# Expert blocks of 56 slots, convolutions that read PSUM, and a reordered VectorE queue in a two-block transformer kernel

## Chip, cores and metric

The kernel runs on one core of one Trainium2 chip. The metric is device time in microseconds (us) of one execution. TensorE is called PE, VectorE DVE, ScalarE ACT, GpSimd POOL and SyncE, which issues the DMAs, SP, as in the profile.

## What is computed

One sequence of 512 tokens with 1024 features passes two blocks, all in fp32. The first block (gated attention, then retention, each with attention to a memory) is not touched. The second block is a mixer and a mixture of experts:

```python
# mixer: three of the projections feed a short convolution, four a gated delta rule with 4 heads of 128
def causal_dwconv(x, w):                 # depthwise over the 512 tokens, K taps
    xp = jnp.pad(x, ((0, 0), (K - 1, 0), (0, 0)))
    y = xp[:, 0:S] * w[0]
    for j in range(1, K):
        y = y + xp[:, j:j + S] * w[j]
...
y = b * causal_dwconv(c * hx, conv_w)                                  # K = 3
qkv = jax.nn.silu(causal_dwconv(concatenate([q, k, v]), conv_w))       # K = 4
q = q * lax.rsqrt(jnp.sum(q * q, axis=-1) + EPS) * (DN_HEAD_DIM ** -0.5)   # k likewise, no factor
...
# experts: 4 groups of 8, each token goes to 2 experts of its best group
yb = (jax.nn.silu(xblk @ w_gate[e]) * (xblk @ w_up[e])) @ w_down[e]    # 1024 -> 512 -> 1024
out = zeros((N, D)).at[slot_tok].add(yb * slot_gate[:, None])
```

There are 32 experts, so 1024 assignments of tokens. All expert weights (32 times three matrices of 2 MB) are read from HBM once.

## The kernel before, in words

**Delta-rule layer (938 to 1245 us).** `dn` (line 1065 on) works head by head. `dn_head` (L1229) makes one 128x512 projection at a time for k, q and v into one of four PSUM banks (pool `pacc`, L444), each a product in three fp32r parts (hH/hL by wh/wl). `conv` (L1186) first has ACT copy the bank into a padded SBUF tile `cpad` (L1259), which frees the bank; DVE then scales (L1195) and adds three shifted taps (L1197) in `cy`. After the SiLU and a transpose, ACT squares the head (L1271) and DVE sums the squares by token (L1272). `short_conv` (L1200) uses the same `conv` with 3 taps, its input made by a DVE product. In this layer the order on each engine comes from the framework's scheduler.

**Experts (1258 us to the end).** `moe` (L1415) cuts the slots of all experts into 16 pairs; an expert has CAP = 64 slots, so a pair is 128 rows.

- `route` (L1500) computes, for each token, its two slot numbers `dest`.
- `build_S` (L1638) makes one-hot matrices from `dest` on DVE, 128 tokens by 128 slots at a time: a comparison with an iota (L1656) and a second one added (L1657). A "quad" is four experts (256 slots).
- `gather_T` (L1660) multiplies tokens by one-hots: 8 feature blocks, 4 token tiles, high and low part, 64 matmuls of 256 columns, into `mhT`. It runs in every second pair; the first stands before pair 0.
- `slot_rows` (L1699) spreads `dest` over the partitions with 16 matmuls, kept as 16-bit `rows`. `slots` (L1709) makes from them the transposed one-hots `ST` of a pair, two comparisons and two comparisons with addition (L1715, L1716).
- `gates` (L1735) gets the gate weight of each slot: four matmuls of 8 columns against the one-hots and some ten tiny DVE operations.
- `gate_up` (L1758) multiplies one expert's 64 rows with its gate and up weights (32 matmuls of 512 columns in two halves), `act_T` (L1793) transposes and forms h (L1802, L1803), `down` (L1806) multiplies by the down weights in two halves of the pair, `y_out` splits the result, and `combine` adds it to the tokens: 16 matmuls of 512 columns and 8 DVE additions (L1852).
- Weights come in tiles of 1 MB through 18 buffers: NWA = 12 and NWB = 6. SP issues a load when a buffer is free (L1767, L1812).
- `spill` (L1597) makes a table of experts with more than CAP tokens, for `overflow` (L1858), a loop at the end that runs once for each block of the table.

In this stage PE's order is written out (`self.pe = self.ordered(nc.tensor)`). For a pair p it is: gate and up of expert 0; down half 1 of pair p-1; the transposes; first half of gate and up of expert 1; combine of p-1; second half; the gather, if there is one; the gate products of p+1; down half 0; transposes of expert 1. DVE and ACT follow the scheduler, which starts work as early as its operands allow, unless `after(a, b)` (L216) sets a behind b on their engine. `sums` shows what DVE is given at the combine:

```python
def sums():
    if p:
        self.combine(blks[p - 1], [(t, n) for n in range(2) for t in range(NT)])
    self.slots(blks[p])
    if more and p % 2:
        self.build_S(quads[p // 2 + 1])
    if not p:
        ov.extend(self.spill(mc))
```

Of the kernel before, what the change touches and what calls it, by code (L numbers as in the profile page):

```python
# [22 lines left out]
P = 128  # L23
# [12 lines left out]
CAP = 64  # L36
NPAIR = NE // 2
SLOTS = NE * CAP
MAXOV = 16
# [3 lines left out]
NWB = 6  # L43
# [11 lines left out]
CM = ["ones", "iota", "ustrict", "eend", "pcol"]  # L55
# [8 lines left out]
def constants():  # L64
# [4 lines left out]
    c["ones"] = np.ones((P, P))  # L69
# [23 lines left out]
    c["pcol"] = np.stack([i, (i + CAP) % P], 1) - P  # L93
# [30 lines left out]
class Model:  # L124
# [689 lines left out]
    def out_router(self, W, heads):  # L814
# [13 lines left out]
        cm = self.rtp.tile([P, sum(self.off[k][1] for k in CM)], F32, tag="cm", name="cm")  # L828
        nc.sync.dma_start(cm, A["cm"])
        iota = self.const(cm, "iota")  # L830
        self.io3 = rp.tile([P, 2, CAP], F32, tag="io3", name="io3")
        V.tensor_copy(self.io3.rearrange("p a n -> p (a n)"), iota)
# [4 lines left out]
        V.tensor_copy(self.onesb, self.const(cm, "ones"))  # L837
        V.tensor_copy(self.ustb, self.const(cm, "ustrict"))
        V.tensor_copy(self.eend, self.const(cm, "eend"))
        V.tensor_scalar(out=self.e64b, in0=self.eend[0:1, :], scalar1=float(-CAP), scalar2=None, op0=ALU.add)  # L840
        self.pcol = rp.tile([P, 2, NPAIR], F32, tag="pcol", name="pcol")
        ends = self.eend.rearrange("p (n e) -> p n e", e=2)[:, None, :NPAIR, 1]
        nc.gpsimd.tensor_tensor(self.pcol, ends.to_broadcast([P, 2, NPAIR]),
                                self.const(cm, "pcol")[:, :, None].to_broadcast([P, 2, NPAIR]), op=ALU.add)
# [341 lines left out]
    def conv(self, wk, src, width, wv):  # L1186

        nc = self.nc
        V = nc.vector
        pad = width - 1  # L1190
        cp = wk.tile([P, S + 3], F32, tag="cpad", bufs=1, name="cpad")
        V.memset(cp[:, :pad], 0.0)
        src(cp[:, pad:pad + S])
        y = wk.tile([P, S], F32, tag="cy", name="cy")
        V.tensor_scalar(out=y, in0=cp[:, 0:S], scalar1=wv(0), scalar2=None, op0=ALU.mult)  # L1195
        for j in range(1, width):
            V.scalar_tensor_tensor(out=y, in0=cp[:, j:j + S], scalar=wv(j), in1=y, op0=ALU.mult, op1=ALU.add)  # L1197
        return y

    def short_conv(self, wk, ct, Wr, C):  # L1200
# [3 lines left out]
        for i in (2, 0, 1):  # L1204
# [4 lines left out]
        y = self.conv(wk, lambda d: V.tensor_tensor(d, pss[1], c, op=ALU.mult), 3,  # L1209
                      lambda j: aw[:, j * 4 + ct:j * 4 + ct + 1])  # L1210
# [18 lines left out]
    def dn_head(self, wk, h, Wr, C, sc, pre):  # L1229
# [23 lines left out]
        for n, (nm, c0) in enumerate(DNC):  # L1253
# [5 lines left out]
            y = self.conv(wk, lambda d: SC.activation(d, ps, AF.Copy), 4, lambda j: cw[:, j * 12 + ci:j * 12 + ci + 1])  # L1259
# [11 lines left out]
            SC.activation(sq, v4(pt), AF.Square)  # L1271
            V.tensor_reduce(ss[:, n * NT:(n + 1) * NT], sq, axis=AX.X, op=ALU.add)  # L1272
# [142 lines left out]
    def moe(self, psd):  # L1415
# [9 lines left out]
        io3 = self.io3  # L1425
        et = mc.tile([P, NPAIR, 1], F32, tag="et", name="et")
        blks = []
        quads = [dict(base=float(q * 2 * P), io=io3, n=2 * P) for q in range(NPAIR // 2)]
        for p in range(NPAIR):
            w = {}  # L1430
            for j in range(2):
                for n, src in (("g", "w_gate_2"), ("u", "w_up_2"), ("d", "w_down_2")):
                    w[n, j] = A[src][0, 2 * p + j]
            nc.gpsimd.tensor_scalar(out=et[:, p, :], in0=self.hm64[:, 1:2], scalar1=float(2 * p), scalar2=None, op0=ALU.add)
            blks.append(dict(pair=p, quad=quads[p // 2], cols=slice(p % 2 * P, (p % 2 + 1) * P), w=w, n=2,
                             e=et[:, p, :], cut=p == NPAIR - 1))
        nb = NPAIR
        self.quad0 = quads[0]
        self.route(mc)
        for q in quads:  # L1440
            q["dest"] = self.dest
# [5 lines left out]
        self.gather_T(quads[0], True)  # L1447
        self.slot_rows()
        blks[0]["first"] = True
        ov = []  # L1450
        for p in range(nb):
            more = p + 1 < nb

            def sums():
                if p:
                    self.combine(blks[p - 1], [(t, n) for n in range(2) for t in range(NT)])
                self.slots(blks[p])
                if more and p % 2:
# [12 lines left out]
            self.gate_up(blks[p], 1, half=sums if more else lambda: self.act_T(blks[p], 0))  # L1471
            if more:
                if not p:
                    self.act_T(blks[0], 0)
# [20 lines left out]
        self.overflow(mc, wk, io3, gb, ot, *ov)  # L1495

    def route(self, mc):
# [30 lines left out]
        iota = self.io3[:, 0, :]  # L1528
# [32 lines left out]
        self.quad0["dest"] = self.dest = dest  # L1561
        self.rt = (oh, ohf, sl, ge, q, sc[3], onesb)

        self.build_S(self.quad0)
# [30 lines left out]
        G.tensor_tensor(self.gxs[:, :, 4:8], gx, self.gxs[:, :, 0:4].bitcast(F32), op=ALU.subtract)  # L1595

    def spill(self, mc):  # L1597
# [11 lines left out]
        for m in range(2, 8):  # L1609
# [3 lines left out]
        V.memset(ones, 1.0)  # L1613
# [4 lines left out]
        for i in range(MAXOV):  # L1618
            cmp = sc[:, (8 + i % 2) * NE:(9 + i % 2) * NE]
# [18 lines left out]
    def build_S(self, blk):  # L1638
# [3 lines left out]
        S3 = wk.tile([P, NT, 2 * P], F32R, tag="S3", name="S3")  # L1642
        iof = blk["io"].rearrange("p a n -> p (a n)")
        ds = []
        for n in range(blk["n"] // P):
            dest = blk["dest"]
            if n or not isinstance(blk["base"], float) or blk["base"]:
                db = wk.tile([P, 2 * NT], F32, tag=f"db{n}", name="db")
                V.tensor_scalar(out=db, in0=dest, scalar1=blk["base"] + n * P if n else blk["base"], scalar2=None,
                                op0=ALU.subtract)  # L1650
                dest = db
            ds.append(dest)
        for t in range(NT):
            for n, dest in enumerate(ds):
                o = S3[:, t, n * P:(n + 1) * P]
                V.tensor_scalar(out=o, in0=iof, scalar1=dest[:, t:t + 1], scalar2=None, op0=ALU.is_equal)  # L1656
                self.last = V.scalar_tensor_tensor(out=o, in0=iof, scalar=dest[:, NT + t:NT + t + 1],  # L1657
# [3 lines left out]
    def gather_T(self, blk, first=False):  # L1661
# [4 lines left out]
        hT = blk["hT"] = wk.tile([P, KD, 2 * P], F32, tag="mhT", name="mhT")  # L1666
        pss = {}

        def mms(k, t, start):
            if k // 2 not in pss:  # L1670
                pss[k // 2] = self.att()
            o = pss[k // 2][:, k % 2 * 2 * P:k % 2 * 2 * P + n]
            for c, part in enumerate(self.xs):
                self.mm(o, part[:, t, k, :], S3[:, t, :n], start and c == 0,
                        t == NT - 1 and c == 1 and (not first or k % 2 == 1))

        def put(b):
            pv = pss[b].rearrange("p (k n) -> p k n", k=2)[:, :, :n]
            o = hT[:, 2 * b:2 * b + 2, :n]
            if b % 2:  # L1680
                nc.vector.tensor_tensor(o, pv, self.gv[:, 2 * b:2 * b + 2, None].to_broadcast([P, 2, n]), op=ALU.mult)
            else:
                for k in range(2):
                    nc.scalar.activation(o[:, k, :], pv[:, k, :], AF.Copy, scale=self.gv[:, 2 * b + k:2 * b + k + 1])

        if first:
            for t in range(NT):
                for k in range(KD):
                    mms(k, t, t == 0 and k % 2 == 0)
                    if t == NT - 1 and k % 2:  # L1690
                        put(k // 2)
        else:
            for k in range(KD):
                for t in range(NT):
                    mms(k, t, t == 0)
                if k % 2:
                    put(k // 2)

    def slot_rows(self):  # L1699

        self.rows = self.wk.tile([P, 2, S], U16, tag="rows", name="rows")
        for i in range(2):
# [4 lines left out]
            self.nc.vector.tensor_scalar(out=self.rows[:, i, :], in0=ps, scalar1=60000.0, scalar2=None, op0=ALU.min)  # L1707

    def slots(self, blk):  # L1709
# [3 lines left out]
        for s, o in enumerate(blk["ST"]):  # L1713
            c = self.pcol[:, s, blk["pair"]:blk["pair"] + 1]
            V.tensor_scalar(out=o, in0=self.rows[:, 0, :], scalar1=c, scalar2=None, op0=ALU.is_equal)  # L1715
            V.scalar_tensor_tensor(out=o, in0=self.rows[:, 1, :], scalar=c, in1=o.bitcast(F32), op0=ALU.is_equal,  # L1716
                                   op1=ALU.add)

    def slot_T(self, blk):
# [3 lines left out]
        for t in range(NT):  # L1723
            self.tr(ps[:, t * P:(t + 1) * P], self.of(blk, "S3")[:, t, :].bitcast(F32))
        blk["ST"] = [wk.tile([P, S], F32R, tag=f"ST{s}", name=f"ST{s}") for s in range(2)]
        SC.activation(blk["ST"][0], ps, AF.Copy)
        for i in range(2):
            SC.activation(blk["ST"][1][(1 - i) * CAP:(2 - i) * CAP, :], ps[i * CAP:(i + 1) * CAP, :], AF.Copy)

    @staticmethod  # L1730
    def of(blk, name):

        return blk["quad"][name][:, :, blk["cols"]]

    def gates(self, blk):  # L1735
# [4 lines left out]
        S3 = self.of(blk, "S3")  # L1740
        for t in range(NT):
            self.mm(ps[:, :8], S3[:, t, :], self.gxs[:, t, :], t == 0, t == NT - 1)
        a = wk.tile([P, 8], F32, tag="ga", bufs=2, name="ga")
# [4 lines left out]
        gt = wk.tile([P, 4], F32, tag="gt", bufs=2, name="gt")  # L1748
# [235 lines left out]
```

## Time and profile before

| | |
|---|---|
| median of 3 runs | 1773.61 us (1772.92 to 1774.19) |
| profiled execution | 1773.5 us |
| its span | 1771.7 us |
| busy: PE, DVE, ACT, POOL | 1724.4, 1007.2, 590.6, 96.6 us |
| chain that ended last | PE 89%, DVE 6%, ACT 2%, DMA 2% |

The span goes from the first to the last instruction. An engine that is idle costs something only where the chain passes through it. The two stages touched by the change have different limits, so their windows are to be read apart.

### The profile page before, as it was taken

Reading aid. Unit: us, or ns where it says so; the run is one execution under the profiler, and the core shown is the slowest. Engines: PE = TensorE matmul, PEld = TensorE weight load, DVE = VectorE, ACT = ScalarE, POOL = GpSimd, SP = SyncE. Lnnn points to the kernel's source line nnn. Section 1 sums busy time; section 2 is a strip of 40 time slices with the busy share of each in tenths; the row PEclk is TensorE's granted clock in tenths of the full one; section 3 lists DMA queues with packets and bytes.
Section 4 is the critical chain, followed back from the end, with each engine's and each line's share of the span. In section 5 each row is a group of like instructions: output and inputs, shape, how many; then the busy total and the mean of one; then the engine's idle time right before and its main releaser. Section 6 shows DMA issues by size and latency. Waiting matters only on the chain.

```text
span 1771.7 us, 24714 instructions
## 1 busy us (share of the span) xinstructions
PE 1724.4 (97%) x9410; PEld 1255.9 (71%) x9410; DVE 1007.2 (57%) x2660; ACT 590.6 (33%) x1173; POOL 96.6 (5%) x143
## 2 busy tenths in 40 slices
PE   8999999999999999999999999999999999999996
PEld 7888888878888888888888777778644445354443
DVE  7655564563757555454657978875545435453534
ACT  7643333433536232222446433334211111111112
POOL 0000000000000110111011000010200000000001
PEclk9999999999999999999999999999999999999998
DMA  8633233233223322223213342326799999999981
GB/s 260 175 96 90 81 93 95 73 86 96 69 92 99 92 85 82 84 75 103 76 48 81 91 111 62 85 69 265 301 418 418 410 409 420 407 407 407 420 321 49
DMA packets 199276, 318.82 MB, mean 180 GB/s; under 512 B 18789, under 2 KB 159590, under 8 KB 174450
## 3 DMA queue, kind: packets, MB, share of 16 engines
q1 hardware_dynamic: 199154, 317.21, 50.6%
q8 instruction: 75, 1.23, 0.3%
q14 instruction: 47, 0.39, 0.1%
HBM read 312.16 MB, written 5.01 MB: 179 GB/s over the span
## 4 chain that ended last, share of the span: by engine, by line
PE 89%; DVE 6%; ACT 2%; DMA 2%; issue 1%; SPq 0%; POOL 0%; POOLq 0%; ACTq 0%; DVEq 0%
PE acc L143 50%; PE pg L230 13%; PE att L143 8%; PE att L230 7%; PE pd L230 6%; PE trp L148 3%; PE trp L230 1%; PE trp L143 1%; DVE wl L205 1%; ACT wh L204 1%; DMA raw<-in_w_mem_kv_dram 1%; DVE cy L1197 1%; PE att L148 0%; ACT hH L243 0%; DMA kvf<-kvd 0%
## 5 line engine op out<-in xcount | busy, mean ns | idle before, releaser
L205 DVE TENSOR_TENSOR wl<-raw,wh 128x1024 fp32r<-128x1024 f32 x184 | 225.8, 1227 | 189.8 <-ACT wh L204 179.8
L143 PE MATMUL acc<-hH,wh 128*128 128x512 f32 (+1 forms) x760 | 297.3, 392 | 5.4 <-DVE sz L578 3.1
L143 PE MATMUL acc<-hL,wh 128*128 128x512 f32 (+1 forms) x760 | 299.1, 394 | 0.0
L143 PE MATMUL acc<-hH,wl 128*128 128x512 f32 (+1 forms) x760 | 298.0, 392 | 0.0
L204 ACT ACTIVATE wh<-raw 128x1024 fp32r<-128x1024 f32 x184 | 194.6, 1059 | 276.8 <-PE acc L143 262.2
L230 PE MATMUL pg<-mw,mhT 128*64 128x512 f32 x1024 | 230.3, 597 | 0.0
L143 PEld LDWEIGHTS acc<-hH,wh 128*128 128x128 f32 x760 | 143.7, 190 | 31.4 <-DVE sz L578 3.3
L143 PEld LDWEIGHTS acc<-hL,wh 128*128 128x128 f32 x760 | 144.0, 189 | 25.4
L143 PEld LDWEIGHTS acc<-hH,wl 128*128 128x128 f32 x760 | 144.0, 189 | 25.4 <-issue 1.0
L230 PEld LDWEIGHTS pg<-mw,mhT 128*64 128x64 f32 x1024 | 69.3, 137 | 129.8 <-issue 129.6
L143 PE MATMUL acc<-wh,hL 128*128 128x256 f32 (+1 forms) x384 | 129.5, 338 | 0.4 <-DVE hL L247 0.4
L143 PE MATMUL acc<-wh,hH 128*128 128x256 f32 (+1 forms) x384 | 129.3, 337 | 0.1
L143 PE MATMUL acc<-wl,hH 128*128 128x256 f32 (+1 forms) x384 | 129.3, 337 | 0.0
L143 PE MATMUL acc<-wh,oh 128*128 128x512 f32 x320 | 127.1, 397 | 1.4 <-ACT oh L243 1.4
L143 PE MATMUL acc<-wl,oh 128*128 128x512 f32 x320 | 126.4, 395 | 0.0
L143 PE MATMUL acc<-wh,ol 128*128 128x512 f32 x320 | 126.2, 395 | 0.0
L230 PE MATMUL pd<-mw,h 128*64 128x512 f32 (+1 forms) x544 | 116.7, 571 | 3.0 <-DVE h L1803 3.0
L1784 ACT ACTIVATE gu<-pg,gt 128x512 f32<-128x512 f32 x32 | 22.0, 687 | 266.7 <-PE pg L230 252.9
L1843 DVE TENSOR_TENSOR yl<-pd,yh 128x512 fp32r<-128x512 f32 x30 | 19.3, 687 | 137.0 <-ACT yh L1842 137.0
L1852 DVE TENSOR_TENSOR x<-att,x 128x512 f32<-128x512 f32 x120 | 73.1, 683 | 31.6 <-PE att L230 31.6
L230 PEld LDWEIGHTS pd<-mw,h 128*64 128x64 f32 x544 | 37.4, 137 | 66.3 <-issue 60.9
L143 PEld LDWEIGHTS acc<-wh,hH 128*128 128x128 f32 x384 | 73.0, 190 | 8.3 <-ACT hH L243 0.8
(567 smaller groups left out, 2863.3 us busy)
## 6 DMA issues: line engine op xcount, KB each, us to landing
mw<-in_w_gate_dram SPq DMA_DIRECT2D x64, 1024.0 KB
mw<-in_w_up_dram SPq DMA_DIRECT2D x64, 1024.0 KB
mw<-in_w_down_dram SPq DMA_DIRECT2D x62, 1024.0 KB
raw<-in_fox_w_in_dram SPq DMA_DIRECT2D x56, 512.0 KB
raw<-in_w_out_dram SPq DMA_DIRECT2D x40, 512.0 KB
raw<-in_w_in_dram SPq DMA_DIRECT2D x28, 512.0 KB
raw<-in_ret_w_in_dram SPq DMA_DIRECT2D x20, 512.0 KB
raw<-in_w_mem_kv_dram SPq DMA_DIRECT2D x16, 512.0 KB
```

The source lines that it names most:

```text
L143: self.pe.matmul(o, l, r, start=start, stop=stop)
L148: self.pe.transpose(o, i, self.ident[b:b + n, b:b + n])
L204: nc.scalar.activation(h, raw, AF.Copy)
L205: nc.vector.tensor_tensor(l, raw, h.bitcast(F32), op=ALU.subtract)
L230: ins = getattr(eng, name)(*a, **k)
L1197: V.scalar_tensor_tensor(out=y, in0=cp[:, j:j + S], scalar=wv(j), in1=y, op0=ALU.mult, op1=ALU.add)
L1784: nc.scalar.activation(gu, pg.rearrange("p (n k) -> p k n", k=4), AF.Copy, scale=blk["us"][:, j:j + 1])
L1843: V.tensor_tensor(l, pd, h.bitcast(F32), op=ALU.subtract)
L1852: self.nc.vector.tensor_tensor(xv, ps, xv, op=ALU.add)
```

## The change

1. **56 slots.** CAP is 56. The row tile of the expert products stays 64 (RT), so these matmuls keep their shapes; an expert's 64 columns overlap its neighbour's, and the added constants `pcol` and `ucol` say which rows count. One gather serves eight experts (an "octet", 448 columns), in pairs 3, 7 and 11 and before pair 0. NWB is 4.
2. **One-hots.** Each token tile of an octet is made in two halves of 224 columns from a 16-bit iota.
3. **Gates on DVE.** The gate products on PE go. `slot_rows` also spreads the gate weights (`grow`, 16 more matmuls and two ACT copies), and `gates` compares, multiplies and sums over 512 columns in four DVE operations. The old form stays as `gates_any` for `overflow`.
4. **Order.** `slots` goes behind the last addition of the combine, an octet's one-hots behind the last operation of `slots`, `gates` behind what was last then. `slot_rows` moves behind the first product of pair 0, `spill` to the end of pair 0. In pair 14 the transposes stand in the middle of the down product.
5. **Delta-rule layer.** `conv` reads PSUM: ACT writes the last tap scaled into `cy`, DVE adds the three others straight from the bank. For k and q, ACT's squares sum themselves, four operations of 128 columns.
6. **Constants and POOL.** The router's constants come in three smaller DMAs; POOL loses the making of `pcol` and 16 small operations, and gains four small ones.

```diff
-CAP = 64
+CAP = 56
+RT = 64
+OCT = 8 * CAP
...
-NWB = 6
+NWB = 4
...
-    def conv(self, wk, src, width, wv):
+    def conv(self, wk, x, width, wv):
...
-        cp = wk.tile([P, S + 3], F32, tag="cpad", bufs=1, name="cpad")
-        V.memset(cp[:, :pad], 0.0)
-        src(cp[:, pad:pad + S])
         y = wk.tile([P, S], F32, tag="cy", name="cy")
-        V.tensor_scalar(out=y, in0=cp[:, 0:S], scalar1=wv(0), scalar2=None, op0=ALU.mult)
-        for j in range(1, width):
-            V.scalar_tensor_tensor(out=y, in0=cp[:, j:j + S], scalar=wv(j), in1=y, op0=ALU.mult, op1=ALU.add)
+        nc.scalar.activation(y, x, AF.Copy, scale=wv(width - 1))
+        for d in range(1, width):
+            nc.vector.scalar_tensor_tensor(out=y[:, d:], in0=x[:, :S - d], scalar=wv(width - 1 - d), in1=y[:, d:],
+                                           op0=ALU.mult, op1=ALU.add)
...
-            y = self.conv(wk, lambda d: SC.activation(d, ps, AF.Copy), 4, lambda j: cw[:, j * 12 + ci:j * 12 + ci + 1])
+            y = self.conv(wk, ps, 4, lambda j: cw[:, j * 12 + ci:j * 12 + ci + 1])
...
-            SC.activation(sq, v4(pt), AF.Square)
-            V.tensor_reduce(ss[:, n * NT:(n + 1) * NT], sq, axis=AX.X, op=ALU.add)
+            for t in range(NT):
+                SC.activation(sq[:, t, :], v4(pt)[:, t, :], AF.Square, accum_out=ss[:, n * NT + t:n * NT + t + 1])
...
-        self.gather_T(quads[0], True)
-        self.slot_rows()
+        self.gather_T(octs[0], True)
...
-                self.slots(blks[p])
-                if more and p % 2:
-                    self.build_S(quads[p // 2 + 1])
-                if not p:
-                    ov.extend(self.spill(mc))
+                self.slots(blks[p], self.last)
+                if more and p % 4 == 3:
+                    self.build_S(octs[p // 4 + 1], self.last)
 
             self.gate_up(blks[p], 0, not p, None if more else sums)
             if not p:
+                self.slot_rows()
                 self.gates(blks[0])
...
-                if p % 2:
-                    self.gather_T(quads[p // 2 + 1])
-                self.gates(blks[p + 1])
-                self.down(blks[p], 0)
-                self.act_T(blks[p], 1)
+                if p % 4 == 3:
+                    self.gather_T(octs[p // 4 + 1])
+                self.gates(blks[p + 1], self.last)
+                self.down(blks[p], 0, (lambda: self.act_T(blks[p], 1)) if p + 2 == nb else None)
+                if p + 2 < nb:
+                    self.act_T(blks[p], 1, "rt" if p else "hx")
+                if not p:
+                    ov.extend(self.spill(mc, self.last))
...
-        S3 = wk.tile([P, NT, 2 * P], F32R, tag="S3", name="S3")
+        S3 = wk.tile([P, NT, OCT], F32R, tag="S3", name="S3")
...
+                if last:
+                    self.after(i, last)
...
+        io = self.ioh[:, :n]
         for t in range(NT):
...
+            for h, d in enumerate(ds):
+                o = S3[:, t, h * n:(h + 1) * n]
+                V.tensor_scalar(out=o, in0=io, scalar1=d[:, t:t + 1], scalar2=None, op0=ALU.is_equal)
+                self.last = V.scalar_tensor_tensor(out=o, in0=io, scalar=d[:, NT + t:NT + t + 1],
                                                    in1=o.bitcast(F32), op0=ALU.is_equal, op1=ALU.add)
...
+        self.grow = self.wk.tile([P, 2, S], F32, tag="grow", name="grow")
+        for i in range(2):
+            ps = self.att()
+            for t in range(NT):
+                for h in range(2):
+                    self.mm(ps[h * RT:(h + 1) * RT, t * P:(t + 1) * P],
+                            self.gr[:, t, i, h:h + 1].to_broadcast([P, RT]), self.ident, True, True)
+            self.nc.scalar.activation(self.grow[:, i, :], ps, AF.Copy)
...
+    def gates(self, blk, last=None):
...
+                x = V.scalar_tensor_tensor(out=junk, in0=self.rows[:, i, :], scalar=self.ucol[:, j, blk["pair"]:blk["pair"] + 1],
+                                           in1=self.grow[:, i, :], op0=ALU.is_equal, op1=ALU.mult,
+                                           accum_out=a[:, i, j:j + 1])
+                if last:
+                    self.after(x, last)
+        us = wk.tile([P, 2], F32, tag="us", bufs=2, name="us")
+        self.last = V.tensor_tensor(us, a[:, 0, :], a[:, 1, :], op=ALU.add)
...
-            self.nc.vector.tensor_tensor(xv, ps, xv, op=ALU.add)
+            self.last = self.nc.vector.tensor_tensor(xv, ps, xv, op=ALU.add)
```

## Rows read from the trace of the kernel before

**Rows 1.** The page: busy time of each engine, its share of the span, instructions.

```profile
PE 1724.4 (97%) x9410; PEld 1255.9 (71%) x9410; DVE 1007.2 (57%) x2660; ACT 590.6 (33%) x1173; POOL 96.6 (5%) x143
```

**Rows 2.** Windows, expert stage: length, busy by engine, clock, DMA share, GB/s.

```profile
1380.89:1407.78 26.89, 26.89 (x127) 10.73 (x128) 11.86 (x30) 2.90 (x6) 0.00 (x0) 1.00 0.99 402
1407.78:1442.19 34.41, 34.41 (x190) 18.26 (x192) 15.83 (x49) 5.01 (x11) 0.00 (x0) 1.00 1.01 421
```

**Rows 3.** Timeline, pair with gather: start us, us, engine line operation.

```profile
1365.76 0.39 PE L230 MATMUL att<-yh,ST 128*128 128x512 f32 x1
...
1365.96 4.88 DVE L1852 TENSOR_TENSOR x<-att,x 128x512 f32<-128x512 f32 x8 [2.10 <-PE att L230]
1365.99 0.40 PE L230 MATMUL att<-yl,ST 128*128 128x512 f32 x1
...
1370.75 0.87 DVE L1715 TENSOR_SCALAR ST<-rows,pcol 128x512 fp32r<-128x512 uint16 x2
...
1371.54 1.41 DVE L1716 SCALAR_TENSOR_TENSOR ST<-rows,pcol,ST 128x512 fp32r<-128x512 uint16 x2
...
1372.75 0.39 PE L230 MATMUL att<-S,xH 128*128 128x256 f32 x1
...
1380.39 0.50 PE L230 MATMUL trp<-gxs,S 128*128 128x8 f32 x4
...
1380.82 0.65 PE L230 MATMUL pd<-mw,h 128*64 128x512 f32 x2
```

**Rows 4.** Timeline, expert stage, end of the pair before it.

```profile
1345.86 0.61 PE L230 MATMUL trp<-gxs,S 128*128 128x8 f32 x4
...
1346.40 1.08 PE L230 MATMUL pd<-mw,h 128*64 128x512 f32 x4
...
1346.59 0.28 DVE L1656 TENSOR_SCALAR S<-io,db 128x128 fp32r<-128x128 f32 x1
```

**Rows 5.** Timeline, start of the expert stage and first pair.

```profile
1256.87 0.28 DVE L1656 TENSOR_SCALAR S<-io,dest 128x128 fp32r<-128x128 f32 x1
...
1260.54 0.19 DVE L1583 RECIPROCAL r<-r 128x8 f32<-128x8 f32 x1
...
1265.63 1.95 PE L230 MATMUL att<-ident,dest 128*128 128x128 f32 x16
...
1285.09 3.65 PE L230 MATMUL pd<-mw,h 128*64 128x512 f32 x16 [1.66 <-DVE h L1803]
```

**Rows 6.** Timeline, last pair but one.

```profile
1719.83 2.37 PE L230 MATMUL pd<-mw,h 128*64 128x512 f32 x10 [1.38 <-DVE h L1803]
```

**Rows 7.** Lines, delta-rule layer: count, busy us, mean ns, idle before, releaser.

```profile
L1195 DVE TENSOR_SCALAR cy<-cpad,vecs 128x512 f32<-128x512 f32 x16 | 7.7, 481 | 0.6 <-issue 0.3
...
L1272 DVE TENSOR_REDUCE dss<-dtmp 128x4 f32<-128x512 f32 x8 | 5.4, 678 | 2.6 <-ACT dtmp L1271 2.6
...
L1404 ACT ACTIVATE dtmp<-Y 128x128 f32<-128x128 f32 x16 | 4.9, 308 | 3.3 <-DVE Y L1402 3.1
```

**Rows 8.** Lines, same stretch, PE at projections.

```profile
L143 PE MATMUL acc<-hH,wh 128*128 128x512 f32 x200 | 82.9, 414 | 5.3 <-DVE sz L578 3.1 <-ACT cpad L1259 2.2
```

**Rows 9.** Windows, delta-rule layer.

```profile
1038.00:1138.00 100.00, 94.62 (x590) 72.55 (x590) 82.31 (x272) 40.67 (x91) 3.50 (x4) 0.98 0.32 80
1068.00:1078.00 10.00, 7.75 (x32) 5.95 (x31) 8.90 (x21) 3.87 (x6) 0.00 (x0) 0.85 0.39 105
```

**Rows 10.** Timeline, delta-rule layer, one projection and the convolution before it.

```profile
1074.10 0.58 ACT L1259 ACTIVATE cpad<-acc 128x512 f32<-128x512 f32 x1
...
1074.73 0.57 PE L143 MATMUL acc<-hH,wh 128*128 128x512 f32 x1 [2.25 <-ACT cpad L1259]
...
1075.10 0.63 PE L143 MATMUL acc<-hL,wh 128*128 128x512 f32 x1
...
1079.64 0.75 DVE L1197 SCALAR_TENSOR_TENSOR cy<-cpad,vecs,cy 128x512 f32<-128x512 f32 x1
```

**Rows 11.** Waits of SP's queue, 1200 to 1771: us in total, times, longest.

```profile
SPq L1767 <- PE pg L230: 245.5, 55, 22.6
```

More of the change, by code (lines that the diff above doesn't have):

```diff
@@ L92, in constants @@
     c["eend"] = np.broadcast_to(np.tile(CAP * (np.arange(NE) + 1.0), NT)[None, :], (P, NT * NE))
-    c["pcol"] = np.stack([i, (i + CAP) % P], 1) - P
+    e = np.arange(NE)[None, :]
+    row = i[:, None] % RT - np.where(e % 8 == 7, RT - CAP, 0)
+    ec = np.where((row >= 0) & (row < CAP), e * CAP + row, -1).reshape(P, NPAIR, 2)
+    up = i[:, None] >= RT
+    c["pcol"] = np.concatenate([np.where(up, ec[:, :, 1 - n], ec[:, :, n]) for n in range(2)], 1)
+    c["ucol"] = np.concatenate([ec[:, :, n] for n in range(2)], 1)
     c["uincl"] = (i[:, None] <= i[None, :]).astype(float)
@@ L1424, in moe @@
         self.junkp, self.junkt = wk, "mhT"
-        io3 = self.io3
-        et = mc.tile([P, NPAIR, 1], F32, tag="et", name="et")
         blks = []
-        quads = [dict(base=float(q * 2 * P), io=io3, n=2 * P) for q in range(NPAIR // 2)]
+        octs = [dict(base=float(q * OCT), n=OCT) for q in range(NPAIR // 4)]
         for p in range(NPAIR):
@@ L1433, in moe @@
                     w[n, j] = A[src][0, 2 * p + j]
-            nc.gpsimd.tensor_scalar(out=et[:, p, :], in0=self.hm64[:, 1:2], scalar1=float(2 * p), scalar2=None, op0=ALU.add)
-            blks.append(dict(pair=p, quad=quads[p // 2], cols=slice(p % 2 * P, (p % 2 + 1) * P), w=w, n=2,
-                             e=et[:, p, :], cut=p == NPAIR - 1))
+            cols = [min((p % 4 * 2 + j) * CAP, OCT - RT) for j in range(2)]
+            blks.append(dict(pair=p, oct=octs[p // 4], cols=cols, w=w, n=2, cut=p == NPAIR - 1))
         nb = NPAIR
-        self.quad0 = quads[0]
+        self.oct0 = octs[0]
         self.route(mc)
-        for q in quads:
+        for q in octs:
             q["dest"] = self.dest
@@ L1595, in route, with spill @@
         G.tensor_tensor(self.gxs[:, :, 4:8], gx, self.gxs[:, :, 0:4].bitcast(F32), op=ALU.subtract)
-    def spill(self, mc):
+        self.gr = wk.tile([P, NT, 2, 2], F32, tag="gr", name="gr")
+        for i in range(2):
+            G.tensor_copy(self.gr[:, :, i, 0:1], r)
+            G.tensor_tensor(self.gr[:, :, i, 1:2], gx[:, :, 2 * i:2 * i + 1], r, op=ALU.mult)
+    def spill(self, mc, last):
         nc = self.nc
@@ L1612, in spill @@
         ones = sc[:, 3 * NE:4 * NE]
-        V.memset(ones, 1.0)
+        self.after(V.memset(ones, 1.0), last)
         V.tensor_tensor_scan(end, ones, nb, initial=0.0, op0=ALU.mult, op1=ALU.add)
@@ L1714, in slots @@
             c = self.pcol[:, s, blk["pair"]:blk["pair"] + 1]
-            V.tensor_scalar(out=o, in0=self.rows[:, 0, :], scalar1=c, scalar2=None, op0=ALU.is_equal)
-            V.scalar_tensor_tensor(out=o, in0=self.rows[:, 1, :], scalar=c, in1=o.bitcast(F32), op0=ALU.is_equal,
-                                   op1=ALU.add)
+            i = V.tensor_scalar(out=o, in0=self.rows[:, 0, :], scalar1=c, scalar2=None, op0=ALU.is_equal)
+            self.after(i, last)
+            self.last = V.scalar_tensor_tensor(out=o, in0=self.rows[:, 1, :], scalar=c, in1=o.bitcast(F32),
+                                               op0=ALU.is_equal, op1=ALU.add)
     def slot_T(self, blk):
@@ L1866, in overflow @@
         n = nc.values_load(tab[0:1, MAXOV:MAXOV + 1], min_val=0, max_val=MAXOV,
-                           skip_runtime_bounds_check_because="at most 15 blocks of 64 overflow 1024 assignments")
+                           skip_runtime_bounds_check_because="at most 18 blocks of 56 overflow 1024 assignments")
         self.pe = nc.tensor
```

181 lines of the change are left out of this document (88 added, 93 removed).

## The prediction

> **What bounds the kernel now.** I read the page first: TensorE (PE) is busy 1724.4 us of a span of 1771.7, VectorE (DVE) 57% of it [rows 1], and the page's chain of work that ended last runs mostly on PE. So a microsecond counts if it is PE work, or if PE waits for it. The change lies in two stages, and the windows separate them. In the expert stage two pairs of experts, without a gather and with one, take 26.89 and 34.41 us, PE busy in all of it at full clock, DVE in 27.7 of the 61.3, while DMA moves 402 to 421 GB/s at a busy share of 0.99 to 1.01 [rows 2]: PE bound, DMA just behind. In the delta-rule layer PE is busy 94.6 of 100 us and DVE 82.3 [rows 9]; there DVE and the PSUM banks decide when PE starts. PE's program order in the expert stage is written out, so a late operand stops everything behind it.
>
> The profiled execution took 1773.5 us (span 1771.7), against a median of 1773.61; the sum is made on 1773.5. About 0.2%, 3.5 us, can be told from no change.
>
> **Expert stage, PE work.** *Gather.* 64 matmuls of 256 columns run from 1372.75 to 1380.39, 7.64 us, 0.119 each; a combine matmul of 512 columns and the same weight width follows its neighbour after 0.23 [rows 3]. For 448 columns I interpolate 0.119 + 0.75 x 0.111 = 0.202, so 12.9 us for eight experts. Four of these for eight of the old ones: 51.6 - 61.1 = **-9.5**. The gate, up and down products keep their row tile of 64 and cost the same.
> *Gates.* The four small products per pair take 0.43 on a gather pair (1380.39 to 1380.82) [rows 3] and 0.54 on the other [rows 4]; 8 of each: **-7.7**. They become four 512-column DVE operations and one small add, 4 x 0.70 (half of the 1.41 for two of that form [rows 3]) + 0.2 = 3.0 us a pair. DVE has 61.3 - 27.7 free in two pairs, and the gates are next needed after the first half of the down product, so they are hidden; were that cover gone, 16 x 3.0 = 48 us would show.
> *New gate rows.* 16 matmuls beside the 16 that build the slot rows in 1.95 us [rows 5]: **+2.0** on PE. Both sets move behind the first product, where they still cost PE time. Two more ACT copies fall in time when ACT is idle.
> *Start.* The first gather needs four one-hot operations for its first token tile, as before, but each 224 columns wide for 128. 16 operations of 128 columns take 1256.87 to 1260.54, 0.229 each [rows 5]; 512 columns take (0.87 + 1.41 - 0.08 overlap)/4 = 0.55 [rows 3]; so 224 columns are 0.229 + 0.25 x 0.32 = 0.31. Four times 0.08: **+0.35**.
> *Spill and tail.* PE waited 1.66 in the first pair [rows 5] while DVE did the spill table; that now stands behind the pair's activations. I take **-1.0** (0 to -1.66), since DVE has the gate rows' work there instead. In the last-but-one pair PE waited 1.38 for h [rows 6]; with the transposes in the middle of the down product the other half covers it: **-1.4**.
>
> **Expert stage, the wait added.** The slot one-hots go behind the last addition of the combine, the next octet's one-hots behind the last of these, on DVE's queue. Before, the gather's one-hots were made some 20 us early (at 1346.59 for a gather at 1372.75 [rows 3, 4]). Now, in the three pairs with a gather, DVE runs: additions until 1370.84, slots until 1372.95 [rows 3], a shift of dest for each half (0.2), 16 operations x 0.31 = 4.95: done at about 1378.1. PE arrives at 1372.75. The first output block needs all four token tiles; of its 8 matmuls 6 (1.2 us) run inside the wait, so PE is 5.35 - 1.2 + 0.4 (semaphores, restarts) = 4.6 late. Three times: **+13.8**. Behind the waiting gather on PE stand the down product and the next pair, and none of it can run; what is behind the one-hots on DVE (the gates, 3.0) is covered by the 12.9 us of the gather.
> *Clock.* After a wait of 2.25 us in the delta layer a matmul takes 0.63 for 0.39, and a 10 us window has a clock of 0.85 [rows 9, 10], which costs 10 x 0.15 = 1.5. The new wait is longer but broken by matmuls. So 0 to 4.5 for three; with no row nearer than this one for a broken wait I take the middle, **+2**.
> *Buffers.* Weight buffers go from 18 to 16 MB. SP's own waits are for PE to free a buffer (245.5 us at the gate and up loads [rows 11]); PE never waited for a weight. 12.58 MB a pair at 421 GB/s is 29.9 us; PE needs 30.65 now and about (3 x 26.35 + 43.85)/4 = 30.7 with the wait (26.35 is 26.89 less 0.54; the gather pair adds 12.9 and 4.6). So **0**.
>
> **Delta layer.** Removed from DVE: 16 scalings (7.7) and 8 reductions (5.4) [rows 7], 13 us in all. ACT's copy stays one ACT operation; eight squares of 512 columns become 32 of 128 at 0.31 [rows 7] with their accumulators, some 9 us on an engine 40% busy [rows 9]. The taps now read PSUM. A PSUM-reading addition of 512 columns takes 4.88/8 = 0.61, a two-operand SBUF one 0.70 [rows 3], so the read itself costs nothing. The Trainium skill, "VectorE: DVE Perf Modes", section "Rules for kernel authors", would copy a matmul's output to SBUF first when several operations follow. That pays where SBUF operations run faster; By that rule the 36 taps of q, k and v would lose, at most, the step from the 0.40 of a scaling to 0.70, 10.8 us of DVE; the rows show the two-operand form no faster from SBUF than from PSUM, and the measurement decides.
> What the read does cost is the bank. There are four for projections. The one whose copy ended at 1074.68 let PE start at 1074.73, with 2.25 us lost; its last tap ended at 1080.39 [rows 10], 5.7 later. So the next projection would start 5.7 later with DVE's order unchanged. Against it: 13 us of DVE relief, of which PE can get back at most its 5.3 of waits at projections [rows 8]. Bounds: -5 and +8. I take 5 - 3 = **+2**.
>
> **Sum:** -9.5 - 7.7 + 2.0 + 0.35 - 1.0 - 1.4 + 13.8 + 2 + 2 = +0.55. Forecast 1774.0: 18 us of PE work saved and handed back as a wait for one-hots.
>
> **Rivals.**
> *A, the one-hots hold nobody.* If DVE can place them earlier than the addition, or they run so fast that PE finds them, 13.8 and the clock's 2 go: 1758.2, chance 0.22. For: DVE is half idle. Against: the order is forced, and between the last addition (1370.84) and the gather (1372.75) there are 1.9 us for 7 us of DVE work [rows 3].
> *B, slower: the banks.* The place is the projections at 1065 to 1075 of the delta layer, where four banks are held until the third tap. The price is the whole 5.7 and, with another drop of clock (1.5) and no relief, the layer costs 5.7 + 1.5 = 7.2 (to 9 with a second such wait) instead of 2: 1779 to 1783, middle 1781. It decides where the third tap of a projection ends later than the start of the projection four on. For: DVE at 82% of this stage. Against: the scheduler may draw taps forward, and 13 us of DVE work are gone. Chance 0.24.
> *C, DMA bound.* With two buffers fewer, weights could arrive late. At the lowest rate of the stage's windows, 402 GB/s [rows 2], a pair needs 31.3 us, 0.6 more than PE: up to 16 x 0.6 = 10 on the forecast, middle 1779. Against: the 421 of the other window, and 16 tiles are 16 x 30.7 / 12 = 41 us of cover. Chance 0.04. The Trainium skill, "DMA: Bandwidth & Descriptors", section "Where 436 GB/s comes from", sets about 358 GB/s for reads from HBM; a pair would then take 35 us and the stage would be DMA bound already; the 421 GB/s of this trace contradict it.
> *D, an overflow pass.* 56 slots could be too few and the pass over overflowing experts would run; but counting the reference's assignments for these inputs, the fullest expert has 41 tokens. No chance.
>
> **How the numbers follow.** Main case 0.50, within 1768 to 1779 (faster 0.12, same 0.28, slower 0.10). A adds 0.22 to faster, B 0.24 and C 0.04 to slower: 0.34, 0.28, 0.38. The range runs from A's value to B's upper end, 1758 to 1783; what it leaves out is A with the delta layer's gain and B with every stall at its dearest.
>
> **What will show it.** Right: in pairs 3, 7 and 11 (counted from 0), a wait of PE at the gather's first blocks named DVE one-hot, 4 to 5 us; other pairs near 26.4; gathers of 12.9; no small gate products. Wrong: PE starting the gather without a wait (A), PE waits named by taps at projections (B), waits named by weight loads (C), or the gather's matmuls at 0.23, which would leave no gain there.

## The result and the profile after

| | before | after |
|---|---|---|
| median, 6 runs each, beside one another | 1773.9 us | 1765.4 us (1764.6 to 1766.5) |
| ratio | | 0.995, 95% interval 0.994 to 0.9961 |
| profiled execution, its span | 1773.5, 1771.7 us | 1765.3, 1763.5 us |

The kernel became 8.5 us, 0.5%, faster. The forecast was 1774.0, no change. Where the time went is read from two marks in the traces: the first gather product starts at 1248.12 instead of 1258.02, and from there to the end the kernel takes 515.4 us instead of 513.7. So what lies ahead of the experts gained 9.9 us, and the expert stage lost 1.7.

The page's row of busy times answers to [rows 1].

```profile
PE 1714.4 (97%) x9122; PEld 1240.7 (70%) x9122; DVE 1013.7 (57%) x2523; ACT 596.6 (34%) x1219; POOL 91.6 (5%) x130
```

PE has 288 fewer products and 10.0 us less busy time; DVE, with the gates, has 6.5 more.

*Expert stage.* Windows of a pair without and with a gather, from combine to combine (columns as in [rows 2]):

```profile
1326.05:1352.25 26.20, 26.20 (x123) 10.31 (x121) 12.98 (x27) 3.12 (x6) 0.00 (x0) 1.00 1.01 420
1352.25:1397.86 45.61, 43.25 (x186) 23.93 (x185) 20.70 (x49) 5.67 (x10) 0.00 (x0) 0.93 0.90 364
```

A plain pair takes 26.20 for 26.89. A pair with a gather takes 45.6, and PE is idle in 2.4 of it. From one combine to the next all ten plain pairs up to pair 14 take 26.2, and the three with a gather 45.61, 45.11 and 46.00. The timeline of the first of these gathers, as in [rows 3]:

```profile
1359.93 0.24 DVE L1655 TENSOR_SCALAR db<-dest 128x8 f32<-128x8 f32 x2
...
1361.49 0.47 PE L236 MATMUL att<-S,xH 128*128 128x448 f32 x1 [1.61 <-DVE S L1667]
...
1362.70 0.74 PE L236 MATMUL att<-S,xH 128*128 128x448 f32 x1 [0.54 <-DVE S L1667]
...
1364.28 0.81 DVE L1667 SCALAR_TENSOR_TENSOR S<-ioh,db,S 128x224 fp32r<-128x224 uint16 x2
...
1365.14 0.74 PE L236 MATMUL att<-S,xH 128*128 128x448 f32 x1
...
1379.07 0.65 PE L236 MATMUL pd<-mw,h 128*64 128x512 f32 x2
```

The half product ends at 1359.8. The one-hots start only at 1359.93, the last ends at 1365.09, and the seventh product, which needs it, starts at 1365.14. PE's waits have 1.61 and 0.54 on record; from the second of them on the products take 0.74, then 0.57, instead of 0.36. The list of PE's waits from 1300 on shows 8.1 us in nine waits for three gathers:

```profile
PE att L236 <- DVE S L1667: 8.1, 9, 1.6
```

What this list doesn't show is the clock. Windows of 5 us from the first late product on:

```profile
1361.20:1366.20 5.00, 3.96 (x9) 2.27 (x10) 4.96 (x16) 0.00 (x0) 0.00 (x0) 0.63 1.01 419
1366.20:1371.20 5.00, 5.00 (x19) 4.50 (x18) 2.62 (x8) 0.83 (x2) 0.00 (x0) 0.69 1.01 419
```

The granted clock, the third number from the end, is 0.63 and 0.69: PE is partly at the lower of its levels after the broken wait, and 19.26 us go by from the end of the half product to the down product at 1379.07.

The first pair, which answers to [rows 5], and the last pair but one, which answers to [rows 6]:

```profile
1248.12 0.45 PE L236 MATMUL att<-S,xH 128*128 128x448 f32 x1 [0.82 <-DVE S L1667]
...
1261.10 7.09 PE L236 MATMUL pg<-mw,mhT 128*64 128x512 f32 x32
1268.12 2.05 PE L236 MATMUL att<-ident,dest 128*128 128x128 f32 x16
1270.10 1.97 PE L236 MATMUL att<-ident,gr 128*64 128x128 f32 x32
1271.89 7.04 PE L236 MATMUL pg<-mw,mhT 128*64 128x512 f32 x32
...
1280.96 2.37 PE L236 MATMUL pd<-mw,h 128*64 128x512 f32 x10 [1.45 <-DVE h L1829]
```

```profile
1707.83 0.66 PE L236 MATMUL trp<-ident,gu 128*128 128x128 f32 x4
...
1710.40 0.38 ACT L1827 ACTIVATE h<-trp 128x256 f32<-128x256 f32 x1 [3.46 <-PE pd L236]
...
1711.75 1.08 PE L236 MATMUL pd<-mw,h 128*64 128x512 f32 x4 [1.39 <-DVE h L1829]
```

The first gather takes 12.98, the two sets of rows 3.77, and the wait of 1.66 is still 1.45. The wait of 1.38 near the end is 1.39.

*Delta layer.* Windows from 938 to the first gather, before and after (new rows, columns as in [rows 9]):

```profile
938.00:1258.02 320.02, 304.80 (x1889) 244.23 (x1887) 240.34 (x791) 137.70 (x291) 25.87 (x54) 0.99 0.42 129
```

```profile
938.00:1248.12 310.12, 301.41 (x1891) 242.58 (x1889) 229.88 (x750) 145.76 (x353) 20.50 (x39) 1.00 0.42 130
```

PE runs the same number of products (1889 and 1891). Its idle time falls from 15.2 to 8.7 us, its busy time by 3.4 with the clock at 1.00 instead of 0.99; DVE has 10.5 us less to do, ACT 8.1 more. Of its lines, those that answer to [rows 7] (the taps, now from the PSUM bank, and the small squares), and the two longest waits of PE that are left:

```profile
L1201 DVE SCALAR_TENSOR_TENSOR cy<-acc,vecs,cy 128x509 f32<-128x509 f32 x12 | 8.9, 742 | 0.0
...
L1277 ACT ACTIVATE dtmp<-att 128x128 f32<-128x128 f32 x32 | 8.4, 276 | 2.7 <-PE att L154 2.7
```

```profile
PE att L149 <- DMA XX<-ldx: 1.4, 1, 1.4
PE acc L149 <- ACT hH L249: 1.4, 1, 1.4
```

A tap takes 0.74 from PSUM, as it did from SBUF. The waits of PE at projections [rows 8] for a bank are gone altogether.

### The profile page after: what moved, and what is told of

Read it like the earlier page. It is cut to its first block, busy times and chain, and to the rows that moved or that the text cites. A ratio compares the mean times of both kernels' runs of the same rounds, so it can differ in the third digit from the quotient of the medians.

```text
span 1763.5 us, 24032 instructions
## 1 busy us (share of the span) xinstructions
PE 1714.4 (97%) x9122; PEld 1240.7 (70%) x9122; DVE 1013.7 (57%) x2523; ACT 596.6 (34%) x1219; POOL 91.6 (5%) x130
## 4 chain that ended last, share of the span: by engine, by line
PE 87%; DVE 7%; ACT 2%; DMA 2%; issue 1%; SPq 0%; POOL 0%; POOLq 0%; ACTq 0%; DVEq 0%
PE acc L149 50%; PE pg L236 12%; PE att L149 8%; PE att L236 6%; PE pd L236 6%; PE trp L154 3%; PE trp L236 1%; PE trp L149 1%; DVE wl L211 1%; DVE x L1878 1%; DMA raw<-in_w_mem_kv_dram 1%; DVE S L1667 1%; DVE cy L1201 0%; ACT wh L210 0%; PE att L154 0%
## 5 line engine op out<-in xcount | busy, mean ns | idle before, releaser
L1810 ACT ACTIVATE gu<-pg,us 128x512 f32<-128x512 f32 x32 | 22.0, 688 | 258.7 <-PE pg L236 255.6
```

What stands on the lines that cost most here:

```text
L1810: nc.scalar.activation(gu, pg.rearrange("p (n k) -> p k n", k=4), AF.Copy, scale=blk["us"][:, j:j + 1])
```

## The experiments

Each changed the kernel after the change (1765.4) unless it says otherwise; in the table all runs stand with their medians, and with the ratio to the kernel before, run beside them.

| run | median us | ratio, interval |
|---|---|---|
| old convolution and old reductions | 1774.8 | 1.0006 (0.9997 to 1.0016) |
| old reductions alone | 1771.9 | 0.9991 (0.9981 to 1.0001) |
| old convolution alone | 1766.2 | 0.9962 (0.9948 to 0.9976) |
| taps from an SBUF copy | 1765.2 | 0.9956 (0.9940 to 0.9973) |
| the same, with old reductions | 1766.2 | 0.9960 (0.9946 to 0.9974) |
| unread reductions on DVE | 1776.7 | 1.0016 (1.0007 to 1.0026) |
| PE filled ahead of the gather | 1763.2 | 0.9948 (0.9931 to 0.9964) |
| one-hots a pair earlier | 1747.6 | 0.9855 (0.9839 to 0.9872) |
| and gates behind h in pair 14 | 1751.4 | 0.9883 (0.9861 to 0.9905) |
| and a buffer of its own for that h | 1746.4 | 0.9846 (0.9833 to 0.9860) |
| and taps from an SBUF copy | 1746.7 | 0.9841 (0.9827 to 0.9854) |

**The delta layer: which part gained?** First both parts were undone, then each alone.

```diff
-            for t in range(NT):
-                SC.activation(sq[:, t, :], v4(pt)[:, t, :], AF.Square, accum_out=ss[:, n * NT + t:n * NT + t + 1])
+            SC.activation(sq, v4(pt), AF.Square)
+            V.tensor_reduce(ss[:, n * NT:(n + 1) * NT], sq, axis=AX.X, op=ALU.add)
...
-            y = self.conv(wk, ps, 4, lambda j: cw[:, j * 12 + ci:j * 12 + ci + 1])
+            y = self.conv(wk, lambda d: SC.activation(d, ps, AF.Copy), 4, lambda j: cw[:, j * 12 + ci:j * 12 + ci + 1])
```

> The changed kernel with the convolution (padded SBUF copy, scaling on DVE) and the sum of squares (reduction on DVE) as before; expert stage as changed. Theory (the 10.1 us between 938 and the out projection come from these two alone): 1765.4 + 10 = 1775.5, first gather at 1258. Rival (they come from elsewhere, constants or POOL work that left, or the scheduler's order): 1765 to 1770.

1774.8, and the first gather stands at 1258.55 again: the two parts are all of it. PE's waits for banks, between 1000 and 1200, came back with the values of before:

```profile
PE acc L149 <- DVE sz L584: 3.1, 1, 3.1
...
PE acc L149 <- ACT cpad L1268: 2.3, 1, 2.3
```

> The changed kernel with only the sum of squares back on DVE (8 reductions of 0.68 us, 8 squares of 512 columns on ACT). Theory (DVE's load sets PE's start in this layer, a microsecond of DVE for one of PE): 5 us of DVE come back, 1770.4. Rival (the removed copy counts, which stood between bank and taps): no difference, 1765.5. Third (ACT's 32 small squares cost more than they save): faster, 1763.

> The changed kernel with only the convolution as before (padded copy, scaling on DVE, taps from SBUF); squares summed on ACT. Theory (DVE's load): 16 scalings at 0.40 to 0.48, 6.4 to 7.7 us of DVE, come back: 1771 to 1773. Rival (the copy's place in the chain): all of the 10 us come back, 1775. Rival (banks held by the taps cost something in the changed kernel): less than the DVE load says, 1768.

Old reductions alone cost 6.5 us, more than their 5 us of DVE. The old convolution alone costs 0.8, though it puts more on DVE (16 scalings, 7.7 busy). So "a microsecond of DVE for one of PE" is no rule here. The trace with old reductions shows why, at the very place that rival B named (its execution, 1775.95, is the slowest of ten):

```profile
1068.84 0.68 DVE L1277 TENSOR_REDUCE dss<-dtmp 128x4 f32<-128x512 f32 x1
...
1070.99 0.75 DVE L1201 SCALAR_TENSOR_TENSOR cy<-acc,vecs,cy 128x509 f32<-128x509 f32 x1
...
1071.89 0.77 PE L149 MATMUL acc<-hH,wh 128*128 128x512 f32 x1 [4.53 <-DVE drt L181]
```

The reduction stands on DVE ahead of the taps, the third tap ends at 1071.74, and PE, which needs the bank, starts at 1071.89 after 4.53 us of waiting. In the changed kernel the same tap ended at 1063.5, before PE came to the same product (1064.18):

```profile
1062.75 0.75 DVE L1201 SCALAR_TENSOR_TENSOR cy<-acc,vecs,cy 128x509 f32<-128x509 f32 x1
...
1064.18 0.39 PE L149 MATMUL acc<-hH,wh 128*128 128x512 f32 x1
```

Two runs test that. One frees the bank early, whatever DVE does:

```diff
-            y = self.conv(wk, ps, 4, lambda j: cw[:, j * 12 + ci:j * 12 + ci + 1])
+            cp = wk.tile([P, S], F32, tag="cpad", bufs=1, name="cpad")
+            SC.activation(cp, ps, AF.Copy)
+            y = self.conv(wk, cp, 4, lambda j: cw[:, j * 12 + ci:j * 12 + ci + 1])
```

> The changed kernel, but ACT first copies each q, k or v bank to SBUF and both the scaled last tap and the three other taps read that copy; the bank is free after one ACT operation, as before the change. 12 ACT operations of 0.6 us more. In the changed kernel no projection waits for a tap, so by the theory (taps hold a bank too long only while DVE also does the reductions) nothing is gained: 1765 to 1766. Rival (banks held by taps cost something here too): 1762. Rival (the extra ACT work comes back through the chain): 1768 or more.

> The kernel with only the reductions back on DVE (1771.9, with a wait of 4.5 us for a third tap at 1067 and 2.1 for solver steps) with the same copy of the bank to SBUF. Theory (that kernel loses its 6.5 us to banks held by taps that stand behind the reductions): the 4.5 wait goes, 1766 to 1768. Rival (it loses them to the reductions' place in the chain from transposed head to keys and queries): no change, 1771 to 1772.

Without the reductions the copy changes nothing (1765.2). With them it takes 5.6 of the 6.5 us away (1766.2), and the wait of 4.5 is gone; the longest at a projection is

```profile
PE acc L149 <- ACT cpad L1265: 2.0, 1, 2.0
```

The other run gives DVE the work of the reductions without their place in the chain from head to keys:

```diff
+            if nm != "v":
+                jo = self.sm.tile([P, NT], F32, tag="jo", name="jo")
+                self.after(V.tensor_reduce(jo, bc(self.ident[:, None, :]), axis=AX.X, op=ALU.add), i)
```

> The changed kernel with 8 reductions of 512 elements of a constant (about 0.68 us each) put on DVE just behind the SiLU product of each k and q head; nobody reads them. As much DVE work as the reductions that the change removed, in nearly the same place, without their place in the chain. Theory (DVE's load, through the taps behind it): 1770 to 1772. Rival (the chain): 1765 to 1766.

1776.7, more than the theory's upper number, with the wait of 4.5 at the same projection:

```profile
1072.64 0.75 DVE L1201 SCALAR_TENSOR_TENSOR cy<-acc,vecs,cy 128x509 f32<-128x509 f32 x1
...
1073.54 0.76 PE L149 MATMUL acc<-hH,wh 128*128 128x512 f32 x1 [4.48 <-DVE drt L181]
```

So the wait comes from DVE's work ahead of the taps, and not from the reductions' place in the chain. The 11 us are not the price of that work, though: the run is late before the layer begins. The same addition near the end of the first block, which the edit doesn't touch, in the changed kernel and in this run:

```profile
917.21 0.69 DVE L790 TENSOR_TENSOR x<-acc,x 128x512 f32<-128x512 f32 x1 [0.59 <-PE acc L149]
```

```profile
923.21 0.69 DVE L790 TENSOR_TENSOR x<-acc,x 128x512 f32<-128x512 f32 x1 [0.59 <-PE acc L149]
```

```profile
0.00:938.00 938.00, 924.89 (x4919) 767.18 (x4920) 526.84 (x1161) 374.82 (x718) 61.80 (x76) 1.00 0.33 97
```

At the same clock and as busy as in the changed kernel, PE gets through 4919 products in these 938 us where that one gets through 4954. Of the 12.4 us by which the first gather is late (1260.56), 6.0 come from there, and 6.4 from the layer, in which its products may be as slow. Why they are slower stays open.

**The expert stage: the wait for one-hots.** The one-hots were made one pair earlier.

```diff
-                if more and p % 4 == 3:
+                if p % 4 == 2 and p + 2 < nb:
                     self.build_S(octs[p // 4 + 1], self.last)
```

> The next octet's one-hots are made one pair earlier, behind the slots of pairs 2, 6 and 10 instead of 3, 7 and 11; nothing else changes. Theory (PE waits for late one-hots and the clock falls in the broken wait): from the end of the product before a gather to the down product behind it the changed kernel takes 19.3 us (1359.8 to 1379.07) against 13.0 for the first gather, so 6.3 at each of three gathers go: 1765.4 - 19 = 1746.5. Rival (DVE's work is only moved: 6 us of one-hots in the pair before delay its gates and h, and PE waits there): half of it comes back, 1755 or more, with PE waits named h or gates in pairs 2, 6 and 10.

1747.6, 17.8 us less. The gather now follows the half product at once, and takes 13.28 from 1367.78 to 1381.06; all three pairs take 39.63 for 45.1 to 46.0.

```profile
1364.20 3.65 PE L236 MATMUL pg<-mw,mhT 128*64 128x512 f32 x16
1367.78 0.47 PE L236 MATMUL att<-S,xH 128*128 128x448 f32 x1
...
1381.06 1.08 PE L236 MATMUL pd<-mw,h 128*64 128x512 f32 x4
```

PE waits nowhere in the pairs before, so DVE's work was only in the wrong place. To part the wait from the clock, PE was given 23 unread products ahead of each late gather:

```diff
+            if n == OCT:
+                pw = self.att()
+                for i in range(23):
+                    self.mm(pw, self.xs[0][:, 0, 0, :], self.xs[0][:, 0, 0:4, :].rearrange("p k n -> p (k n)"), True, True)
             for k in range(KD):
```

> The changed kernel with 23 products of 512 columns (0.23 each, 5.3 us) of constant operands into an unread bank ahead of each of the three later gathers, so that PE is busy until the one-hots are there. Theory (of 6.3 us lost per gather 5.2 are the wait and the rest the clock, which falls in the broken wait): the gather then runs at full speed behind 5.3 us of filling, 18.2 for 19.3 from product to product, 1765.4 - 3 = 1762. Rival (the clock is no cause; the slow gather is bound by something else): each gather is 12.9 to 14 us behind the filling and 1765 or more, since the first six products no longer run inside the wait.

1763.2, but by the ratios (intervals 0.9931 to 0.9964 here, 0.994 to 0.9961 for the changed kernel) that is no clear gain. The trace:

```profile
1359.11 5.51 PE L236 MATMUL att<-xH 128*128 128x512 f32 x23
1364.45 0.37 PE L236 MATMUL att<-S,xH 128*128 128x448 f32 x1
...
1377.77 1.08 PE L236 MATMUL pd<-mw,h 128*64 128x512 f32 x4
```

```profile
1364.10:1369.10 5.00, 5.00 (x26) 4.52 (x25) 3.99 (x11) 0.63 (x1) 0.00 (x0) 1.00 1.01 421
```

5.34 us of filling, then 13.32 for the gather at a clock of 1.00, 18.66 in all, the same in all three pairs (45.01 or 45.02). The changed kernel takes 45.61, 45.11 and 46.00, together 1.7 us more. In the traces of the six other runs that have the late one-hots, such a pair takes 44.78 to 46.63. So a kernel that does nothing useful for 5.3 us is about even with one that starts the gather in pieces, and mostly a little ahead. In the first such pair of the changed kernel 58 products were left at 1365.14; at the spacing of this run, (1377.77 - 1364.45)/64 = 0.208, they need 12.1 us, and took 13.9: the clock cost 1.8 in this gather, the wait itself 4.2 (6.0 in all, 19.26 against 13.28).

**A faster version.** Two more edits went for the wait of 1.39 in pair 14.

```diff
-                self.gates(blks[p + 1], self.last)
-                self.down(blks[p], 0, (lambda: self.act_T(blks[p], 1)) if p + 2 == nb else None)
+                if p + 2 < nb:
+                    self.gates(blks[p + 1], self.last)
+                self.down(blks[p], 0, (lambda: self.act_T(blks[p], 1)) if p + 2 == nb else None)
+                if p + 2 == nb:
+                    self.gates(blks[p + 1], self.last)
```

> The kernel with one-hots made one pair early (1747.6), and in pair 14 the gates of pair 15 put behind the second activation of pair 14 on DVE instead of ahead of it. Theory: the wait of 1.39 for h in pair 14, which the change left as it was although it put the transposes into the middle of the down product, is there because four gate operations (3.3 us) stand ahead of h on DVE; without them the other half of the down product (1.9 us) covers h and the wait goes: 1747.6 - 1.4 = 1746.2. Rival (1.4 is the activation's own time, as in pair 0): 1747.6, with the same wait.

The wait stayed, 1.40, so the gates in front of h were not its cause:

```profile
1692.13 0.66 PE L236 MATMUL trp<-ident,gu 128*128 128x128 f32 x4
...
1694.70 0.38 ACT L1830 ACTIVATE h<-trp 128x256 f32<-128x256 f32 x1 [3.46 <-PE pd L236]
...
1696.05 1.51 PE L236 MATMUL pd<-mw,h 128*64 128x512 f32 x6 [1.40 <-DVE h L1832]
```

ACT's tanh waits for PE's down product, though its transposes are over at 1692.79. `act_T` writes h into one buffer (tag "rt") for both experts of a pair, and the down product that was to cover the activation reads the first expert's h from it. With the other tag for this one call:

```diff
-                self.down(blks[p], 0, (lambda: self.act_T(blks[p], 1)) if p + 2 == nb else None)
+                self.down(blks[p], 0, (lambda: self.act_T(blks[p], 1, "hx")) if p + 2 == nb else None)
```

> The kernel with one-hots a pair early and gates behind h in pair 14, where h of expert 1 now has a buffer of its own (the one that pair 0 uses). In the run before, ACT's tanh for it waited until 1694.70 for the half of the down product that reads the same buffer, although its transposes had ended at 1692.79. Theory (the buffer is the wait): no wait of PE for h in pair 14, 1.4 us less in the expert stage than in that run, about 1746.2 where the delta layer keeps its clock. Rival (another operand is late): a wait of more than 0.5 stays there.

```profile
1689.72 0.66 PE L236 MATMUL trp<-ident,gu 128*128 128x128 f32 x4
...
1690.31 5.37 PE L236 MATMUL pd<-mw,h 128*64 128x512 f32 x24
1690.42 0.38 ACT L1830 ACTIVATE h<-trp 128x256 f32<-128x256 f32 x1 [1.58 <-PE trp L236]
```

The tanh starts at 1690.42, and the 24 products of both halves run on without a wait; from the combine of pair 14 to that of 15 it takes 18.60 us for 20.21. The buffer without the moved gates was not run. The median, 1746.4, is 1.5% under the kernel before. Runs of these versions spread more than their edits explain: 1747.4 to 1755.4, 1748.3 to 1754.3, 1745.6 to 1751.4. In the profiled execution of 1755.4 a wait of the delta layer is followed by a low clock:

```profile
1029.93 1.08 PE L149 MATMUL att<-XX,E 128*128 128x64 f32 x8 [1.77 <-DMA XX<-ldx]
```

```profile
1030.00:1040.00 10.00, 10.00 (x70) 7.54 (x70) 5.14 (x25) 1.59 (x3) 0.00 (x0) 0.56 0.34 81
1040.00:1050.00 10.00, 10.00 (x64) 7.05 (x64) 5.30 (x28) 1.42 (x3) 0.52 (x1) 0.76 0.16 48
```

> The same with the taps of q, k and v read from an SBUF copy of the bank. Runs of the kernel with early one-hots spread from 1747.4 to 1755.4, and in the slowest PE's granted clock was 0.56 in the 10 us after a wait of 1.8 for a transfer of the solver (at 1029.9). With the copy that wait was not there (under 0.4 us). Theory (the spread is the clock after this wait): the spread shrinks to 2 us or so, median 1745 to 1747. Rival (the spread comes from elsewhere): still 5 us or more between fastest and slowest.

With the SBUF copy (the edit shown above) that wait is gone, the clock is 1.00 from 1000 to 1050, and the runs lie between 1745.95 and 1747.26.

```profile
1000.00:1050.00 50.00, 48.91 (x305) 37.88 (x303) 42.12 (x149) 22.89 (x52) 2.85 (x2) 1.00 0.44 112
```

That the spread is the clock behind this wait is likely, but not shown. Without the copy four of the five runs lie as close (1745.6 to 1746.9), and the kernel after the change, with the same wait (1.44), has six runs within 1.9 us. In the execution of 1755.4, 1.9 us of the 8 were already lost ahead of the layer (the addition of 917.21 starts at 919.1).

## Why the prediction was wrong

The time was out by 8.6, within the range, but on the side of "faster", which had 0.34. That it fell into the range is luck: the low end was there for rival A, which did not occur, and the gain came from the layer for which a loss was forecast. Step by step:

| step | forecast | measured |
|---|---|---|
| gathers, without wait | -9.5 | -7.1 |
| gates off PE | -7.7 | -10.5 |
| new gate rows | +2.0 | +1.9 |
| start | +0.35 | +0.3 |
| spill | -1.0 | -0.2 |
| wait in pair 14 | -1.4 | 0 |
| wait for one-hots, with clock | +15.8 | +17.8 |
| delta layer | +2 | -10.2 |

(Gathers: seven of 34.42 - 26.88 = 7.54 and the first of 7.61 against three of 39.63 - 26.20 = 13.43 and the first of 12.98. Gates: 0.68 a pair, 13 times, 0.51 and 1.1 at the two ends. Wait: 45.61 + 45.11 + 46.00 - 3 x 39.63. The start is the difference of the waits of 0.82 and 0.5 ahead of the first gather, so the 9.9 is split into +0.3 and -10.2. The measured steps add up to -8.0; the spans differ by -8.2.)

**The step that failed is the delta layer's, "5 - 3 = +2".** It measured -10.2, outside even its own bounds of -5 and +8. It made two errors. The 5 was the hold of the bank "with DVE's order unchanged"; but the change took 10.5 us off the very queue on which the taps stand, so the third tap came before PE did. The mechanism exists, 4.5 us at the named place, but only where reductions, or as much unread work, stand on DVE ahead of the taps. And the 3 was capped by "its 5.3 of waits at projections". Those waits hung on DVE's lateness: the 3.1 us name DVE, and the copy that PE awaited for 2.25 us stands on ACT behind `th`, which waits for DVE's third tap:

```profile
1072.78 0.75 DVE L1197 SCALAR_TENSOR_TENSOR cy<-cpad,vecs,cy 128x512 f32<-128x512 f32 x1
```

```profile
1073.56 0.63 ACT L1261 ACTIVATE th<-cy 128x512 f32<-128x512 f32 x1 [0.21 <-DVE cy L1197]
```

And the cap left out the clock and the shorter waits: idle time fell by 6.5 us, busy time by 3.4. I had read the clock of 0.85 and the 2.25 us of waiting beside each other and counted the clock only as a loss, for the new wait and in rival B, and not as something that the relief gives back. The two parts don't add up either: from the layer as it was before (1774.8), the squares alone give 8.6, the convolution alone 3.0, both 9.4.

**The expert stage was right in kind.** From the first gather on -1.8 was forecast for it and +1.7 measured. The one-hots came late by the mechanism and in the three pairs named, and the wait was all but the size given (4.2 for 4.6), while the clock took some 1.8 a gather where I had 0.7. Rival A's reason against itself held: the order is forced. The gates saved more than the four small products, since 0.68 goes and these were 0.43 to 0.54. Two small steps fell for one reason: the wait of 1.4 between a transpose and the down product is the activation's own time on ACT and DVE, not the spill in pair 0, and not covered in pair 14, where h had no second buffer. The gather of eight experts takes 13.4 in the loop against 12.9 by interpolation; in the first it is 12.98.

**Rivals.** C did not occur: PE has no wait for a weight, at 420 GB/s in a plain pair. The taps take 0.74 from PSUM as from SBUF, which agrees with the rows that the prediction set against a rule: reading the bank costs nothing, holding it can cost 5.6. The Trainium skill, "VectorE: DVE Perf Modes", section "Rules for kernel authors", advises either to accept "1× (PSUM src)" or to copy from PSUM to SBUF first if many operations follow. In the kernel with the reductions the copy did pay (1766.2 for 1771.9), though by the bank and not by the speed of the operations.

## What to carry to other kernels

Where PE waits for an engine that is four fifths busy, work taken off that engine can come back in full, with the clock that the waits cost, but by its place and not by its amount: here 10.5 us off DVE gave 10.2, while the convolution's part alone gave 0.8 with the squares moved and 3.0 without. Price the change on the new queue, not on the old one's timetable. An operand's maker that is ordered behind other work needs its finish time set against its user's arrival: here one line, a pair earlier, was worth more than twice the whole change. Work moved into the middle of a product is covered by its second half only if it writes a buffer which that half doesn't read.

## What was not expected of the hardware

A wait cut into pieces by single products was followed by a granted clock of 0.63 and 0.69 over 10 us, so that filling the whole wait with unread products was a little faster in the changed kernel's first late gather: 18.66 us against 19.26. The same wait of the delta layer was followed by a clock of 1.00 in one execution (1.44 us, kernel after) and of 0.56 in another (1.77 us), but of 1.00 again in the kernel before (1.92 us); the runs of the kernel with early one-hots differ by up to 8 us, of which this may be 6.
